# Common pool offsets, a composed pooling matrix, a selection rate of 0.78 and an earlier first load in a one-core encoder block

## The chip, the cores and the metric

The kernel runs on one core of one Trainium2 chip. The metric is the device time of one execution in microseconds (us). Engines are named as in the profile: PE (TensorE: matmuls, and PEld, its weight loads), DVE (VectorE), ACT (ScalarE), POOL (GpSimd) and SP (SyncE, which here only issues DMAs).

## The reference, cut to what matters

One layer of a hybrid encoder block over 2048 tokens of width 1024, in fp32. What the change touches is the pooling branch:

```python
proj = x @ w_in[l]
q, c_kv, q_idx, w_idx, k_idx, pool_in, gate_logits = split(proj)
attn = sparse_indexed_attention(q, k_lat, c_kv, q_idx, w_idx, k_idx)   # top 256 keys per query
branch_a = (attn per head @ w_uv) @ w_attn_branch[l]
# multiscale_pool: per group g of 128 channels, trailing mean over (2,4,8,16)[g] frames minus token
mixed    = einsum('bsgc,gcd->bsgd', pooled, w_pool) * pool_scale
branch_b = mixed @ w_pool_branch[l]
gate_a, gate_b = split(sigmoid(gate_logits))
x = LN(ALPHA*x + (gate_a*branch_a + gate_b*branch_b) @ w_out[l])
x = LN(ALPHA*x + conv_ffn(x))
```

Between the pooled values and `branch_b` there is nothing that is not linear: a 128x128 map per group, a scale per channel, and a 512x1024 matrix.

## The kernel before, in words

**Arithmetic.** Every fp32 operand is split into two fp32r parts, high and low (`split`, `split_new`): either ACT writes the high part and DVE the low part of the whole tile, or POOL does both in pieces of 256 columns. `mm3` (L346) then makes one product of three matmuls: high by high, high by low, low by high. Its second operand is the stationary one or the moving one as the caller wants; in a row of the profile `p<-x,b` the moving operand is in `x`, the stationary one in `b`.

**Stages, in order of time.** Four groups of 512 tokens each pass through `proj_index` (about 0 to 204 us: the indexer's rows and keys), then, in a second round, each group through `proj_pool`, `proj_q` and `proj_gates` (about 204 to 1061 us). Attention over 16 blocks of 128 queries follows (to about 1620 us), then `mix_out` (to about 1900 us), then the feed-forward part in two halves, `up_half` and `down_half` each (to the end).

**The background.** Index scores and the bitwise top-256 selection (`scores_and_selection`) run in the background of the projections. They are generators on the list `bg`; `turn` (L368) is called between pieces of foreground work and takes steps from them while a credit lasts. The credit grows by `RATE` times the modelled PE time that went by, and a step costs the modelled DVE or ACT time that it emits, whichever is more. `widen` (L1124), called in the last gate stage of the last group, emits all that is left of the background at once, releases the pool `wide` that holds the index scores, and opens the pool `more` in the same place. All engines execute in the order in which the program emits; SP issues its DMAs in that order too.

**Weights.** `Weights.get(i)` (L257) hands out the split parts of weight i, loads i+1 and i+2 and splits i+1. In group 0 the parts are split on chip and also stored to a DRAM scratch (`keep`, the DMAs `wp<-b`); groups 1 to 3 load them back from there. Of the splits that may go to POOL every fourth by a running count of all splits (`turns`) goes to ACT and DVE.

**The pooling branch.** `proj_pool` makes the four groups' inputs, `window` their trailing sums on POOL, and `less` the pooled values, split in two. In `tables`, at the start, the 128x128 maps `w_pool` are loaded and split into the tile `wpool`. In `proj_gates`, at the four places `PM_AT` = (4, 5, 6, 7) of the gate loop, `pool_map(k)` (L799) multiplies pooled group k by its map, and ACT and DVE scale and split the result into `self.pm`. Later, for each of four j, 24 matmuls of 512 columns multiply `self.pm` by 256 columns of `w_pool_branch`, whose load and split `self.ab` does like any other weight. So a group has four calls of `pool_map`, three matmuls each.

**Where the tiles lie.** Tiles come from pools that stand one behind the other in each partition's memory. From the left: `const`, `big` (tile name `b`, made by `T`), `mid` (`m`), `sm`, and then `wide` (index scores, `i`) and later `more` (`x`) in the same place. From the right end: `early` (among others `kst`, the indexer's keys), and later `late` (`l`) in its place. As the program before places them, a tile of `big` or `mid` begins at byte 96 modulo 512 in its partition, one of `wide` or `more` at byte 160, `kst` at 416, `wpool`, `cos` and `sin` at 480, and one of `late` at 480. Slices taken of them by the matmuls of the projections, of attention's values, of the mix and of the feed-forward part step by multiples of 512 bytes. The identity matrix used for transposes lies at 128. In `up_half` the weights are in `b`; the activations that they multiply lie, by X_MORE and `x_mix`, in `b`, `x` or `l`.

**The first pool weights.** In `proj_index` of the last group, after the loop over x of its first weight block, `self.ab.split(0)` loads and splits the first two blocks of the pooling projection.

Of the kernel before, what the change touches and what calls it, by code (L numbers as in the profile page):

```python
# [9 lines left out]
F32 = mybir.dt.float32  # L10
F32R = mybir.dt.float32r
# [4 lines left out]
AF = mybir.ActivationFunctionType  # L16
OP = mybir.AluOpType
# [3 lines left out]
P = 128  # L21
NB = S // P
G = 512
NG = S // G
# [48 lines left out]
FINE = "fine"  # L73
PAUSE = "pause"
GRAIN = 1
RATE = 0.75
CAP = 1.5
TAIL = "D--"
ORDER = (3, 2, 1, 6, 5, 4, 7)
# [20 lines left out]
X_MORE = tuple((m, 2) for m in ORDER[:6]) + tuple((m, 3) for m in ORDER[:2])  # L100
LASTK = 8
KEYS_AT = 5
PM_AT = (4, 5, 6, 7)
SCAN = 1.04
PIECE = 256

# [160 lines left out]
class Kern:  # L267
    def __init__(self, ctx, tc, a, out):
        self.clocks = Clocks()
        self.tc, self.nc, self.a, self.out = tc, PacedCore(tc.nc, self.clocks), a, out  # L270
        self.stores, self.older, self.bg, self.late = [], [], [], []
        self.const = ctx.enter_context(tc.tile_pool(name="const", bufs=1))
        self.big = ctx.enter_context(tc.tile_pool(name="big", bufs=34))
        self.mid = ctx.enter_context(tc.tile_pool(name="mid", bufs=8))
        self.sm = ctx.enter_context(tc.tile_pool(name="sm", bufs=4))
        self.early_pool = tc.alloc_tile_pool(name="early", bufs=1, side="right")
        self.wide_pool = tc.alloc_tile_pool(name="wide", bufs=4)
        self.late_pool = self.more_pool = None
        self.p1 = ctx.enter_context(tc.tile_pool(name="p1", bufs=4, space=PSUM))
        self.p2 = ctx.enter_context(tc.tile_pool(name="p2", bufs=2, space=PSUM))  # L280
        self.dram = ctx.enter_context(tc.tile_pool(name="dram", bufs=1, space=bass.MemoryType.DRAM))
        self.n, self.shared, self.turns, self.plain = 0, True, 0, True
        self.credit = self.seen = 0.0
# [119 lines left out]
    def tables(self):  # L403
        nc = self.nc
        posf = self.M([NB, P])
        nc.vector.tensor_copy(posf, self.posi)
        inv = self.E([P, ROT], name="inv")
        for i, f in enumerate(FREQS):
            nc.gpsimd.memset(inv[:, i:i + 1], f)
        pp = self.PS1()  # L410
        nc.tensor.transpose(pp[:, :NB], posf, self.ident[:NB, :NB])
        pos = self.C([P, NB], name="pos")
        nc.vector.tensor_copy(pos, pp[:, :NB])
        self.cos = self.E([P, NB, ROT], name="cos")
        self.sin = self.E([P, NB, ROT], name="sin")
        n = NB * ROT
        ang = self.M([P, NB, ROT])
        nc.vector.tensor_tensor(ang, pos.unsqueeze(2).to_broadcast([P, NB, ROT]),
                                inv[:, None, :].to_broadcast([P, NB, ROT]), op=OP.mult)
        ang = ang.rearrange("p b r -> p (b r)")  # L420
        kf = self.M([P, n])
        for s in (2.0 ** 21, 2.0 ** 10, 1.0):
            nc.vector.tensor_scalar(kf, ang, 1.0 / (2 * math.pi * s), MAGIC, op0=OP.mult, op1=OP.add)
            nc.vector.tensor_scalar(kf, kf, MAGIC, None, op0=OP.subtract)
            for c in TWO_PI:
                nc.vector.scalar_tensor_tensor(ang, kf, -c * s, ang, op0=OP.mult, op1=OP.add)
        for tab, shift in ((self.sin, 0.0), (self.cos, math.pi / 2)):
            r = self.M([P, n])
            nc.vector.tensor_scalar(r, ang, shift, None, op0=OP.add)
            nc.vector.tensor_scalar(kf, r, PI32, -2 * math.pi, op0=OP.is_gt, op1=OP.mult)  # L430
            nc.vector.tensor_tensor(r, r, kf, op=OP.add)
            nc.vector.tensor_scalar(r, r, PI32, -PI32, op0=OP.min, op1=OP.max)
            nc.scalar.activation(tab.rearrange("p b r -> p (b r)"), r, AF.Sin)
        nc.tensor.transpose(pp[:, 16:20], self.psc, self.ident[:4, :4])
        nc.vector.tensor_copy(self.pscale, pp[:, 16:20])
        wp = self.T([P, 4, P])
        nc.sync.dma_start(wp, self.a["w_pool"][0].rearrange("g c d -> c g d"))
        self.wpool = self.E([P, 2, 4, P], F32R, name="wpool")
        self.split(self.wpool[:, 0], self.wpool[:, 1], wp)

    def setup(self):
        nc = self.nc
        self.ident = self.C([P, P], name="ident")
        make_identity(self.tc.nc, self.ident)
        self.mhalf = self.C([P, 1], name="mhalf")
        nc.gpsimd.memset(self.mhalf, -0.5)
        self.ws = self.E([P, NB, IH], name="ws")
        self.kst = self.E([P, S], F32R, name="kst")
        self.halo = self.C([P, 4, HALO], name="halo")
        nc.gpsimd.memset(self.halo, 0.0)  # L450
        self.rcount = self.C([P, HALO], name="rcount")
        for t in range(HALO):
            nc.gpsimd.memset(self.rcount[:, t:t + 1], 1.0 / (t + 1))
        self.pscale = self.C([P, 4], name="pscale")

        self.d_cv = [self.DT([G, DL], name="cv") for _ in range(NG)]
        self.d_xT = [[self.DT([P, 2, 2, G], name="xT") for _ in range(DC // 2)] for _ in range(NG)]
# [108 lines left out]
    def proj_index(self, g, done):  # L566

        nc = self.nc
        rows = [self.T([P, 704]) for _ in range(RB)]
        self.rows[g] = rows  # L570
        for c in range(3):
# [3 lines left out]
            n = 256 if c < 2 else 200  # L575
            if c == 0:
                accs = [self.PS1() for _ in range(RB)]

                def use(pair):
                    for rb in range(RB):  # L580
                        drain(self.proj_r(accs[rb][:, :256], w, rb, 256, [pair]))

                n = 0
                for _ in self.split_x(g, use):
                    if n == (XAT if g else 3) and g + 1 < NG:
                        self.load_x(g + 1)
                    n += 1
                    yield
                if g + 1 == NG:
                    self.ab.split(0)  # L590
                    self.plain = False
                    self.load_parts(0, range(NFIRST))
            for rb in range(RB):
                if c == 0:
                    ps = accs[rb]
                else:
                    if (c, rb) == P1AT and g + 1 < NG:
                        self.split_ahead(g + 1, P1N)
                    ps = self.PS1()
                    yield from self.proj_r(ps[:, :n], w, rb, n)  # L600
                b = g * RB + rb
# [194 lines left out]
        if self.lazy:  # L796
            self.lazy.pop(0)()

    def pool_map(self, k):  # L799
        nc = self.nc  # L800
        t = self.pooled[k]
        ps = self.PS1()
        self.mm3(ps, self.wpool[:, 0, k], self.wpool[:, 1, k], t[:, 0], t[:, 1], True, True)
        o = self.T([P, 2, G], F32R)
        sc = self.pscale[:, k:k + 1]
        nc.scalar.activation(o[:, 0], ps, AF.Identity, scale=sc)
        nc.vector.scalar_tensor_tensor(o[:, 1], ps, sc, o[:, 0].bitcast(F32), op0=OP.mult, op1=OP.subtract)
        self.pm.append(o)

    def proj_gates(self, g):  # L810
        nc = self.nc
        base = g * self.nab + 6
        self.pm = []
        for j in range(4):
            w = self.ab.get(base + j)
            if j == 1:
                self.rope_load(g)
            while self.lazy or j and self.fins:
                self.lazy_step()
            if j == 2:  # L820
                turning = self.rope_turn(g)
            for i in range(2):
                ps = self.PS1()
                for step in self.proj_t(ps, w, i * P):
                    if j == 2:
                        turning.pop(0)()
                    yield step

                def gate(dst=self.d_gm[g][:, 2 * j + i, 0], ps=ps):
                    ga = self.M([P, G])  # L830
                    nc.scalar.activation(ga, ps, AF.Sigmoid)
                    nc.scalar.dma_start(dst, ga)

                self.after(DG, gate)
                if 2 * j + i + 1 in PM_AT:
                    yield 2.6
                    self.pool_map(len(self.pm))
                yield 2.6
        for j in range(4):
            w = self.ab.get(base + 4 + 2 * j)  # L840
# [12 lines left out]
            for i in range(2):  # L853
                ps = self.PS1()
                yield from self.proj_t(ps, w, i * P)

                def gate(ps=ps):
                    gb = self.M([P, G])
                    nc.scalar.activation(gb, ps, AF.Sigmoid)
                    gates.append(gb)  # L860

                self.after(DG, gate)
                if 9 + 2 * j + i in PM_AT:
                    yield 2.6
                    self.pool_map(len(self.pm))
                yield 2.6
            if j == 3 and g + 1 < NG:
                self.load_parts(g + 1, range(NPRE, DC // 2))
# [3 lines left out]
            for i in range(2):  # L872
                ps = self.PS1()
                c0 = i * P
                for k in range(4):
                    self.mm3(ps, wh[:, k, c0:c0 + P], wl[:, k, c0:c0 + P], self.pm[k][:, 0], self.pm[k][:, 1],
                             k == 0, k == 3)
                    if k in FW:
                        yield FINE
# [292 lines left out]
    def scores(self, b, hf):  # L1172
# [8 lines left out]
            del self.qs[b]  # L1181
        N = P * (b + 1)
        npc = (N + 1023) // 1024
        st = self.unit[(b, hf)] = {"p": [], "sum": self.sml([P, 4, 2], tag="ssum", bufs=10), "np": npc}
        cost = 12.0 * N * 0.00042
        for h4 in range(4):
            h = hf * 4 + h4
# [845 lines left out]
```

## Time and profile before

| what | value |
|---|---|
| times of the runs shown | 3251.01, 3256.0, 3257.76 us (median 3256.0) |
| profiled execution, its own time | 3253.0 us |
| its span, first to last instruction | 3251.2 us |
| PE / PEld busy | 3144.5 / 2594.9 us (97% / 80%) |
| DVE / ACT / POOL busy | 2351.4 / 1516.1 / 1238.0 us |
| mean granted PE clock | 0.987 |
| matmuls | 15054 |

Busy times are those of instructions in the trace, and a matmul's end is modelled: two matmuls in a row overlap in it, so PE can be 100% busy and still have matmuls that start later than they could. The distance from one start to the next, or the time of a stretch divided by the number of its matmuls, tells PE's pace. "Idle before" names what an engine waited for before a group of instructions.

### The profile page before, as it was taken

Reading aid. Unit: us, or ns where it says so; the run is one execution under the profiler, and the core shown is the slowest. Engines: PE = TensorE matmul, PEld = TensorE weight load, DVE = VectorE, ACT = ScalarE, POOL = GpSimd, SP = SyncE. Lnnn points to the kernel's source line nnn. Section 1 sums busy time; section 2 is a strip of 40 time slices with the busy share of each in tenths; the row PEclk is TensorE's granted clock in tenths of the full one; section 3 lists DMA queues with packets and bytes.
Section 4 is the critical chain, followed back from the end, with each engine's and each line's share of the span. In section 5 each row is a group of like instructions: output and inputs, shape, how many; then the busy total and the mean of one; then the engine's idle time right before and its main releaser. Section 6 shows DMA issues by size and latency. Waiting matters only on the chain.

```text
span 3251.2 us, 44226 instructions
## 1 busy us (share of the span) xinstructions
PE 3144.5 (97%) x15054; PEld 2594.9 (80%) x15054; DVE 2351.4 (72%) x3947; ACT 1516.1 (47%) x2338; POOL 1238.0 (38%) x1262
## 2 busy tenths in 40 slices
PE   8899899999999899999999999999999999999998
PEld 8887787888888788888778877777878778887786
DVE  4589868978998777777676576666678955555788
ACT  3467547836774666666511133333344522222442
POOL 4126411020010877776631143343176611111663
PEclk9999999999999999999999999999999999999999
DMA  8558855853866444443554358998897666666984
GB/s 302 179 188 291 308 189 206 319 194 126 297 218 221 148 164 140 167 167 138 180 207 162 132 207 311 336 336 295 296 367 256 234 245 243 238 242 232 352 281 163
DMA packets 331809, 753.94 MB, mean 232 GB/s; under 512 B 32122, under 2 KB 117054, under 8 KB 331582
## 3 DMA queue, kind: packets, MB, share of 16 engines
q1 hardware_dynamic: 322774, 735.36, 63.6%
q10 hardware_dynamic: 8808, 15.74, 1.3%
q8 instruction: 119, 1.95, 0.2%
q14 instruction: 108, 0.88, 0.1%
HBM read 518.56 MB, written 232.42 MB: 231 GB/s over the span
## 4 chain that ended last, share of the span: by engine, by line
PE 75%; DVE 10%; DMA 5%; POOL 4%; issue 4%; ACT 2%; SPq 0%; DVEq 0%; ACTq 0%; POOLq 0%
PE p L160 75%; DVE b L160 4%; DVE m L160 3%; POOL b L160 1%; ACT b L160 1%; DMA b<-h 1%; POOL x L160 1%; DMA b<-in_w_ffn_down_dram 1%; POOL l L160 1%; ACT m L160 1%; DMA wp<-b 1%; POOL m L160 1%; DVE h L160 1%; DMA b<-in_w_in_dram 0%; DMA b<-xT 0%
## 5 line engine op out<-in xcount | busy, mean ns | idle before, releaser
L160 PE MATMUL p<-b,b 128*128 128x512 f32 (+2 forms) x9284 | 2231.2, 380 | 67.5 <-DVE b L160 25.2
L160 PEld LDWEIGHTS p<-b,b 128*128 128x128 f32 x9284 | 1647.1, 190 | 403.4 <-DVE b L160 37.4
L160 ACT ACTIVATE b<-p 128x512 fp32r<-128x512 f32 (+9 forms) x662 | 403.8, 634 | 632.7 <-PE p L160 595.8
L160 ACT ACTIVATE b<-b 128x1024 fp32r<-128x1024 f32 (+2 forms) x255 | 261.3, 1029 | 411.1 <-POOL b L160 155.8
L160 DVE TENSOR_TENSOR b<-b,b 128x1024 fp32r<-128x1024 f32 (+4 forms) x261 | 364.0, 1425 | 74.4 <-ACT b L160 67.6
L160 PE MATMUL p<-x,b 128*128 128x512 f32 x1440 | 384.2, 395 | 0.8 <-DVE m L160 0.8
L160 ACT ACTIVATE m<-i,F 128x1536 int8<-128x1536 f32 (+4 forms) x224 | 316.8, 1416 | 65.3 <-DVE F L160 35.7
L160 PEld LDWEIGHTS p<-x,b 128*128 128x128 f32 x1440 | 271.5, 189 | 63.4 <-DVE m L160 1.2
L160 DVE TENSOR_SCALAR_CACHE_REDUCE m<-i,F 128x1152 int8<-128x1152 f32 (+7 forms) x238 | 314.6, 1338 | 1.2 <-DMA gm<-m 0.3
L160 DVE TENSOR_TENSOR m<-m,p 128x512 f32<-128x512 f32 x176 | 120.2, 684 | 263.9 <-ACT b L160 199.1
L160 POOL TENSOR_TENSOR b<-b,b 128x256 fp32r<-128x256 f32 (+3 forms) x212 | 238.7, 1140 | 99.8 <-ACT b L160 91.1
L160 POOL TENSOR_TENSOR m<-b,b 128x512 f32<-128x512 f32 x99 | 137.9, 1401 | 339.6 <-issue 262.0
L160 DVE SCALAR_TENSOR_TENSOR b<-b,cw,b 128x1023 f32<-128x1023 f32 (+1 forms) x176 | 242.9, 1388 | 14.0 <-ACT b L160 13.2
L160 DVE TENSOR_TENSOR b<-p,b 128x512 fp32r<-128x512 f32 (+1 forms) x286 | 201.2, 713 | 69.3 <-ACT b L160 66.8
L160 POOL TENSOR_TENSOR b<-b,m 128x512 f32<-128x512 f32 x110 | 190.4, 1744 | 137.1 <-DMA m<-in_w_ffn_down_dram 85.4
L160 PE MATMUL p<-b 128*128 128x512 f32 x616 | 234.5, 393 | 4.4 <-ACT b L160 3.7
L160 PE MATMUL p<-b,x 128*128 128x512 f32 (+3 forms) x864 | 228.1, 394 | 2.6 <-DVE mx L160 1.6
L160 DVE CUSTOM_DVE_ANT_0 b<-p,b 128x1024 f32<-128x1024 f32 (+7 forms) x192 | 174.1, 909 | 72.9 <-PE p L160 67.4
L160 ACT ACTIVATE m<-p 128x512 f32<-128x512 f32 (+1 forms) x188 | 110.2, 591 | 199.9 <-PE p L160 194.7
L160 PE MATMUL p<-ident,b 128*128 128x128 f32 x1328 | 196.7, 275 | 2.8 <-DVE b L160 1.6
L160 ACT ACTIVATE b<-b,mx 128x1024 f32<-128x1024 f32 (+7 forms) x192 | 171.5, 896 | 53.6 <-DVE mx L160 52.3
L160 DVE SCALAR_TENSOR_TENSOR i<-b,ws,i 128x768 f32<-128x768 f32 (+5 forms) x154 | 159.0, 1061 | 50.3 <-ACT b L160 47.3
(145 smaller groups left out, 3032.7 us busy)
## 6 DMA issues: line engine op xcount, KB each, us to landing
b<-uw SPq DMA_DIRECT2D x308, 512.0 KB, 6.3
b<-wp SPq DMA_DIRECT2D x192, 512.0 KB, 6.1
uw<-l SPq DMA_DIRECT2D x98, 512.0 KB, 3.0
b<-in_w_ffn_down_dram SPq DMA_DIRECT2D x154, 256.0 KB, 5.2
b<-h SPq DMA_DIRECT2D x154, 256.0 KB, 5.3
wp<-b SPq DMA_DIRECT2D x64, 512.0 KB, 6.0
uw<-b SPq DMA_DIRECT2D x56, 512.0 KB, 4.5
h<-m SPq DMA_DIRECT2D x110, 256.0 KB, 5.7
```

Source lines behind the costliest of these rows:

```text
L160: return f(*args, **kw)
```

## The change

Four things are changed together. (1) A pool `edge` with one tile of 384 bytes is placed at the right end, a tile `end` of 448 bytes is added to `early`, and a tag of `sm` gets 8 buffers of 32 bytes where it had 10. (2) `pool_map` is dropped. `w_pool` is loaded in the first gate step of group 0 (`pool_load`), transposed on PE, scaled and split (`pool_turn`); in each of the four j of group 0, `compose` multiplies it into the 256 columns of `w_pool_branch` that are next, in 12 matmuls of 256 columns, and ACT and DVE split the product, which takes the place of the weight. The branch matmuls of all groups then multiply the pooled values by the product; groups 1 to 3 load it back from the scratch. (3) `RATE` is 0.78, it was 0.75. (4) The first pool weights are loaded (not split) before the loop over x of the last `proj_index`.

```diff
-RATE = 0.75
+RATE = 0.78
-PM_AT = (4, 5, 6, 7)
@@ Kern.__init__
+        self.edge = ctx.enter_context(tc.tile_pool(name="edge", bufs=1, side="right"))
         self.early_pool = tc.alloc_tile_pool(name="early", bufs=1, side="right")
@@ tables
-        wp = self.T([P, 4, P])
-        nc.sync.dma_start(wp, self.a["w_pool"][0].rearrange("g c d -> c g d"))
-        self.wpool = self.E([P, 2, 4, P], F32R, name="wpool")
-        self.split(self.wpool[:, 0], self.wpool[:, 1], wp)
@@ setup
+        edge = self.edge.tile([P, 96], F32, tag="edge", name="edge")
+        nc.gpsimd.memset(edge, 0.0)
...
         self.kst = self.E([P, S], F32R, name="kst")
+        nc.gpsimd.memset(self.E([P, 112], name="end"), 0.0)
...
+        self.wpool = self.E([P, 2, 4, P], F32R, name="wpool")
@@ proj_index
             if c == 0:
                 accs = [self.PS1() for _ in range(RB)]
+                if g + 1 == NG:
+                    self.ab.load(0)
@@ in place of pool_map
+    def pool_load(self):
+        self.wp = self.T([P, 4, P])
+        self.nc.sync.dma_start(self.wp, self.a["w_pool"][0].rearrange("g c d -> c g d"))
+
+    def pool_turn(self):
...
+        for k in range(4):
+            nc.tensor.transpose(ps[:, k], self.wp[:, k], self.ident)
+        for k in range(4):
+            sc = self.pscale[:, k:k + 1]
+            nc.scalar.activation(t[:, 0, k], ps[:, k], AF.Identity, scale=sc)
+            nc.vector.scalar_tensor_tensor(t[:, 1, k], ps[:, k], sc, t[:, 0, k].bitcast(F32),
+                                           op0=OP.mult, op1=OP.subtract)
+
+    def compose(self, i):
+        (wh, wl), = self.ab.parts[i]
+        hi, lo = self.T([P, 4, 256], F32R), self.T([P, 4, 256], F32R)
+        for c in range(2):
+            ps = self.PS1([P, 2, 256])
+            for n in range(2):
+                k = 2 * c + n
+                self.mm3(ps[:, n], self.wpool[:, 0, k], self.wpool[:, 1, k], wh[:, k], wl[:, k], True, True)
+            cs = slice(2 * c, 2 * c + 2)
+            nc.scalar.activation(hi[:, cs], ps, AF.Copy)
+            nc.vector.tensor_tensor(lo[:, cs], ps, hi[:, cs].bitcast(F32), op=OP.subtract)
+        self.ab.parts[i] = [(hi, lo)]
@@ proj_gates, first half (j, i)
+            if g == 0 and j == 0:
+                self.pool_load()
...
-                if 2 * j + i + 1 in PM_AT:
-                    yield 2.6
-                    self.pool_map(len(self.pm))
+                if g == 0 and (j, i) == (1, 0):
+                    self.pool_turn()
@@ proj_gates, second half (j, i)
-                if 9 + 2 * j + i in PM_AT:
-                    yield 2.6
-                    self.pool_map(len(self.pm))
+                if g == 0 and i == 0:
+                    self.compose(base + 5 + 2 * j)
...
-                    self.mm3(ps, wh[:, k, c0:c0 + P], wl[:, k, c0:c0 + P], self.pm[k][:, 0], self.pm[k][:, 1],
+                    self.mm3(ps, wh[:, k, c0:c0 + P], wl[:, k, c0:c0 + P], self.pooled[k][:, 0], self.pooled[k][:, 1],
                              k == 0, k == 3)
@@ scores
-        st = self.unit[(b, hf)] = {"p": [], "sum": self.sml([P, 4, 2], tag="ssum", bufs=10), "np": npc}
+        st = self.unit[(b, hf)] = {"p": [], "sum": self.sml([P, 4, 2], tag="ssum", bufs=8), "np": npc}
```

More of the change, by code (lines that the diff above doesn't have):

```diff
@@ L797, in lazy_step @@
             self.lazy.pop(0)()
-    def pool_map(self, k):
+    def pool_load(self):
+        self.wp = self.T([P, 4, P])
+        self.nc.sync.dma_start(self.wp, self.a["w_pool"][0].rearrange("g c d -> c g d"))
+    def pool_turn(self):
         nc = self.nc
[L801 to L808, printed above, removed]
+        ps = self.PS1([P, 4, P])
+        t = self.wpool
+        for k in range(4):
[5 more added lines that the diff above has]
+                                           op0=OP.mult, op1=OP.subtract)
+        self.wp = None
+    def compose(self, i):
+        nc = self.nc
+        (wh, wl), = self.ab.parts[i]
[9 more added lines that the diff above has]
+        self.ab.parts[i] = [(hi, lo)]
     def proj_gates(self, g):
@@ L812, in proj_gates @@
         base = g * self.nab + 6
-        self.pm = []
         for j in range(4):
             w = self.ab.get(base + j)
+            if g == 0 and j == 0:
+                self.pool_load()
             if j == 1:
```

## The prediction

> **What bounds the kernel now.** I read the page first, then the chain of waits in order of time, then PE's timeline where the chain stays on PE, and last the waits around the edges of the stages. Of the page one line, the shares of the chain that ended last:
>
> ```profile
> PE 75%; DVE 10%; DMA 5%; POOL 4%; issue 4%; ACT 2%; SPq 0%; DVEq 0%; ACTq 0%; POOLq 0%
> ```
>
> PE sets the time, so its pace and its waits are all that counts. The chain, in order of time (start, length, number of instructions), shows the pace:
>
> ```profile
> 26.09 80.01 PE p L160 x681
> ...
> 1649.82 175.32 PE p L160 x755
> ...
> 2617.69 386.14 PE p L160 x1660
> ...
> 3059.42 111.38 PE p L160 x490
> ```
>
> All but the first are stretches of 512-column matmuls. In the second down half one takes 111.38/490 = 227.3 ns. In the second up half it takes 386.14/1660 = 232.6 ns, in the mix 175.32/755 = 232.2. The shapes are the same. PE's timeline inside the second up half, and at the step into the down half, shows what differs:
>
> ```profile
> 2746.16 1.55 PE L160 MATMUL p<-b,b 128*128 128x512 f32 x6
> 2747.55 1.55 PE L160 MATMUL p<-x,b 128*128 128x512 f32 x6
> ...
> 3015.85 0.39 PE L160 MATMUL p<-l,b 128*128 128x512 f32 x1
> 3016.08 0.85 PE L160 MATMUL p<-b,b 128*128 128x512 f32 x3
> 3016.77 0.40 PE L160 MATMUL p<-b 128*128 128x512 f32 x1
> ...
> 3021.77 0.62 PE L160 MATMUL p<-b,b 128*128 128x512 f32 x2
> 3022.22 0.39 PE L160 MATMUL p<-b 128*128 128x512 f32 x1
> 3022.45 0.62 PE L160 MATMUL p<-b,b 128*128 128x512 f32 x2
> ```
>
> From start to start: where the moving operand alternates between pools, even matmuls with both operands in `b` take (2747.55-2746.16)/6 = 232 ns. After the last `l` the pace is first (3016.77-3016.08)/3 = 230, and in the pure stretch (3022.45-3021.77)/3 = 226.7. So the loss isn't in the pool `x` itself: it follows each step from one pool to another and lasts some matmuls beyond it. The pools differ in their offset modulo 512 (96, 160, 480). Tiles inside `b` lie 4096 bytes apart over more than 130 KB, so distance alone, at equal offset, doesn't show it.
>
> **The change part by part.** *Offsets.* Reckoned from the places before: `late` goes to 480-384 = 96, `kst` to 416-384-448, again 96 modulo 512, `wide` and `more` to 160-64 = 96. All matmuls of mix and feed-forward then have one offset. Their number:
>
> ```profile
> L160 PE MATMUL p<-x,b 128*128 128x512 f32 x1440 | 384.2, 395 | 0.8 <-DVE m L160 0.8
> L160 PE MATMUL p<-b,x 128*128 128x512 f32 x744 | 206.2, 404 | 0.4 <-DVE mx L160 0.4
> L160 PE MATMUL p<-l,b 128*128 128x512 f32 x396 | 104.4, 403 | 9.2 <-DVE b L160 9.2
> ```
>
> An up half has 22x7x12 = 1848 matmuls, so at 232.6-227.3 = 5.3 ns each at most 9.8 us. I take 9.3 for the second half, and 7 for the first, whose stretches are short and broken by waits after which PE must find its pace again. Mix: at most 755 x (232.2-227.3) = 3.7; only half its moving operands lie in `x`; I take 2.5. Attention: the 744 matmuls with stationary `x`, at most 744 x 5.3 = 3.9; transposes, whose identity stays at 128, come every few matmuls and break the pace anyway; I take 2.5. Keys in `kst`: 0.7, since slices that start at odd multiples of 256 bytes stay off. Sum 22, between 0 (the offset is not the cause) and 28. A loss I exclude: the new offset is the one at which the fast stretches run.
>
> The Trainium skill speaks against this part. In "TensorE: Matmul & The Clock Gate", Part 2, "Step-by-step: what each phase is for", it says that PE has two independent read ports, and that loading the next weights does not steal read bandwidth from the running matmul; by that, an offset between operands is worth nothing. By this rule the sum below would be 22 us higher; by the rows it is as stated.
>
> *Composed matrix.* Out go 48 matmuls of `pool_map`, and in group 1 the waits that come with it:
>
> ```profile
> L160 PE MATMUL p<-b,wpool x48: 392/398/404, 309.5 to 990.0; 128*128 128x512 f32 x48
> ...
> L160 PE MATMUL p<-b,b 128*128 128x256 f32 x960 | 127.8, 290 | 14.8 <-ACT b L160 8.7 <-DVE b L160 3.2 <-POOL b L160 2.7
> ...
> L160 PE MATMUL p<-ident,b 128*128 128x128 f32 x1328 | 196.7, 275 | 2.8 <-DVE b L160 1.6 <-issue 0.9 <-ACT b L160 0.2
> ...
> PE p L160 <- ACT m L160: 5.4, 3, 4.0
> ```
>
> At 227.3 ns they are 10.9 us. In come 4x12 matmuls of 256 columns at 127.8/960 = 133 ns, 6.4 us, and four transposes of 196.7/1328 = 0.15 us: a net 3.9 us less. The 5.4 us (PE's waits from 500 to 700 us) arise because ACT, full of selection passes, is late to empty PSUM, of which each `pool_map` takes a buffer; without it the gates alone hold them, and I count all 5.4 as gone. ACT and DVE lose `pool_map`'s 16 passes each, which lay beside PE's work.
>
> New is that `compose` needs the split weight one gate step (24 matmuls, 5.4 us) earlier than the branch did, in PE's order, so all matmuls queue behind it. In group 0:
>
> ```profile
> 334.76 33.94 PE L160 MATMUL p<-b,b 128*128 128x512 f32 x149
> ...
> 343.50 1.27 DVE L160 TENSOR_TENSOR b<-b,b 128x1024 fp32r<-128x1024 f32 x1 [0.17 <-ACT b L160]
> ...
> 376.37 34.28 PE p L160 x142
> ...
> 400.81 1.51 POOL L160 TENSOR_TENSOR b<-b,b 128x256 fp32r<-128x256 f32 x2
> ```
>
> The stretch of 149 is 5 + 48 + 24 + 48 + 24, so the first `compose` would stand at 334.76 + 29 x 0.227 = 341.3 us; the split ends at 344.8: 3.5 us late. The last one would stand at 376.37 + 94 x 0.227 = 397.7, the split ends at 402.3: 4.6 late. The first delay pushes PE toward a stall that stands at 368 to 376 us anyway and is partly lost in it. I take 4 us, between 0 and 10. The product's own evacuation (ACT, DVE) has the next gate step as cover; without it 1 to 2 us each. Every fourth split changes engine, because one split less is counted: zero, within 4 us either way. Part: -3.9 - 5.4 + 4 = -5.3.
>
> *Rate.* What is left over at the end of the last group is emitted at once by `widen`, and PE meets it:
>
> ```profile
> 1050.76 1.89 ACT L160 ACTIVATE b<-i,tn 128x1920 f16<-128x1920 f32 x1
> 1052.73 1.60 POOL L160 TENSOR_SCALAR x<-b 128x256 fp32r<-128x256 f32 x2 [24.17 <-ACT b L160]
> ...
> 1054.87 4.57 DVE L160 TENSOR_TENSOR_SCAN b<-b 128x1920 f16<-128x1920 f16 x1
> ...
> 1065.09 0.66 PE L160 MATMUL p<-b,b 128*128 128x128 f32 x4 [3.81 <-DVE b L160]
> ...
> PE p L160 <- DVE b L160: 3.8, 1, 3.8
> PE p L160 <- DVE mx L160: 2.6, 4, 1.5
> PE p L160 <- POOL b L160: 1.4, 2, 1.0
> ```
>
> POOL's first split into `x` waits for ACT's last read of `i`, DVE's splits stand behind a selection tail, of which the row of 1054.87 is the last long scan, and PE waits for these (last rows: its waits from 1044 to 1130 us). 0.03 more credit over the 829 us from 216 to 1045, at 0.2153 modelled (L142) for 0.227 real, is 23 us of work, less about 4 for modelled PE time that is gone with `pool_map`: more than a tail of about 15 us. DVE then splits at once, and POOL starts 7 or 8 us sooner. I take 7, between 8 (the three rows of waits) and -3.
>
> *First load.* Now:
>
> ```profile
> 145.65 5.77 DMA b<-in_w_in_dram
> ...
> 156.46 0.98 ACT L160 ACTIVATE b<-p 128x640 f32<-128x640 f32 x2 [4.70 <-POOL b L160]
> 161.27 1.51 ACT L160 ACTIVATE b<-p 128x768 f32<-128x768 f32 x2 [3.84 <-POOL b L160]
> ...
> PE p L160 <- ACT b L160: 6.4, 2, 3.5
> ```
>
> The load lands at 151.4, POOL splits until 161, and ACT's score tiles wait for buffers that POOL still reads; PE waits 6.4 us for ACT (its waits from 150 to 165 us). Issued one weight block earlier, by some 12 us, the load lands and is split before ACT needs these buffers; On SP it passes some stores of scratch and one load of an index row, each of which moves back by the two issues of this load, under 2 us; the scores have that much in hand. It holds two buffers of `big` for those 12 us more. Between 0 and 6.4, I take 5. The load of `w_pool` leaves the start, where PE runs without a break (26.09, 80.01 us), so nothing; in group 0 it is asked for three gate steps, some 16 us, ahead of its transposes, and in SP's order its one issue delays what follows by under 1 us.
>
> **Sum.** 22 + 5.3 + 7 + 5 = 39.3. Against the profiled execution's own 3253.0 us this gives 3213.7; the median of the runs shown is 3.0 above that one, so 3217.
>
> **The rivals.** (a) Offset without effect; for it, another stage may be slower for another reason, its many short accumulations say; against it, the return to 226.7 ns within some ten matmuls of the last foreign operand. 3217 + 22 = 3239. This is the result of the skill's rule on read ports, too.
>
> (b) Offsets and first load come, but group 0's new waits (10 in place of 4) and a selection that ends no sooner take the rest. The 5.4 us of waits for ACT stay, so the composed matrix costs -3.9 + 10 = 6: 3256 - 22 - 5 + 6 = 3235. For it: POOL works in order, and its last split above ends 4.6 us after the place where PE would want it; against it, the stall at 368 to 376 takes up part of what comes before.
>
> (c) Slower: at 0.78 the selection outruns DVE and ACT, and PE waits for gate evacuations behind it.
>
> ```profile
> 560.00:700.00 140.00, 139.09 (x606) 114.97 (x607) 128.97 (x303) 90.07 (x122) 19.74 (x28) 0.99 0.71 260
> 780.00:1030.00 250.00, 250.00 (x1102) 205.27 (x1101) 231.28 (x414) 179.01 (x202) 14.10 (x21) 1.00 0.63 228
> 290.00:420.00 130.00, 117.69 (x495) 95.31 (x494) 111.47 (x294) 71.39 (x131) 63.08 (x109) 0.95 0.89 325
> ```
>
> DVE is at 128.97/140 = 92% and 231.28/250 = 93%. Four per cent more selection, less the passes of `pool_map`, makes 94 to 95: it fits. If the idle 7% cannot be filled, since a selection pass waits for the decision of the one before, the 4% come back as waits over 755 us: 30 us, and the granted clock falls with waits (0.95 from 290 to 420, 6.5 us of 130), some 15 more, and the 7 of the rate are lost: 3256 - 32 + 45 = 3269. It decides from the point where DVE's idle share is all chain.
>
> (d) All four small and cancelling: about 3253.
>
> **How the numbers follow.** Forecast 0.62 (3200 to 3232 by its bounds), (a) 0.12, (b) 0.16, (c) 0.06, (d) 0.04. Range 3198 to 3244: it holds forecast, (a) and (b). About 0.2% is what a measurement of this kernel can tell from no change. Faster by more: 0.62 + 0.12 + 0.16, less tails, 0.88; within: 0.05; slower: 0.07.
>
> **What would show it.** Offsets: the second up half at 227 ns a matmul (about 377 us for 1660) where it is 232.6; if it stays, (a). Composition: no PE wait for ACT at 550 to 561; waits before 256-column matmuls in group 0. Rate: POOL's first split into `x` with no long scan on DVE beside it, and PE unbroken there; DVE over 95% with PE waits for ACT or DVE between 560 and 1030 would be (c). First load: no ACT wait for POOL at 156 and 161. The prediction is wrong if the span is above 3241 or if the feed-forward part isn't shorter by 10 us or more.

## The result

| | before | changed | |
|---|---|---|---|
| median (6 executions each) | 3255.0 us | 3230.1 us | ratio 0.9915 [0.9905, 0.9925] |
| profiled execution, own time | 3253.0 us | 3230.6 us | -22.4 us |
| PE busy | 3144.5 us | 3123.2 us | -21.3 us |

The change makes the kernel faster by 24.9 us in the medians (27.7, between 24.4 and 30.9, by the ratio and its interval). The forecast was 3217, 39 us less than before. The total is inside the predicted range and on its slow side; the terms of the sum are another matter.

The changed kernel's page, its span and its busy times:

```profile
span 3228.8 us, 44242 instructions
PE 3123.2 (97%) x15058; PEld 2590.6 (80%) x15058; DVE 2352.2 (73%) x3941; ACT 1511.3 (47%) x2332; POOL 1245.5 (39%) x1272
```

PE still sets the time. Where the 22 us went is read by lining up the same foreground matmul in both traces and following the difference of its start: -0.8 us at the first pool projection (204 us); +31.3 where group 1's projections start (410.5 before, 441.8 after), of which some 8 are 32 score matmuls and 16 transposes that now come ahead of this point; +9.1 where group 2's start, +5.7 where group 3's start; +1.8 just ahead of attention; -8.4 twenty microseconds into it; -8.2 at its end; -10.1 at the end of the mix; -17.8 at the end of the first up half, -16.1 where the second starts; -21.1 at its end; -22.4 at the end. So group 0 takes, and the later groups, attention's start and the two up halves give. The busy times by stage say the same; columns are the stretch in us, its length, then for PE, PEld, DVE, ACT and POOL the busy us with the number of instructions, then the granted clock, the DMA share and GB/s. The kernel before:

```profile
204.00:432.00 228.00, 210.06 (x895) 169.65 (x894) 194.57 (x542) 136.25 (x257) 118.87 (x208) 0.96 0.83 297
432.00:1040.00 608.00, 601.17 (x2710) 493.92 (x2709) 522.82 (x958) 401.36 (x504) 50.58 (x65) 1.00 0.60 215
1040.00:1130.00 90.00, 80.95 (x431) 68.40 (x429) 66.08 (x173) 50.55 (x118) 70.57 (x75) 0.92 0.48 150
```

The changed kernel, the same stretches:

```profile
204.00:432.00 228.00, 197.66 (x827) 154.78 (x825) 196.24 (x538) 136.91 (x261) 121.57 (x208) 0.93 0.75 266
432.00:1040.00 608.00, 608.00 (x2762) 503.98 (x2762) 520.39 (x952) 393.67 (x487) 52.31 (x68) 1.00 0.63 226
1040.00:1130.00 90.00, 86.84 (x484) 73.60 (x483) 62.40 (x178) 53.22 (x127) 75.69 (x80) 0.98 0.53 167
```

From 204 to 432 us PE now idles 30 us of 228 where it idled 18, and its granted clock is 0.93 instead of 0.96. From 432 to 1040 it has no gap at all (608.00 of 608.00). From 1040 to 1130 it idles 3 us instead of 9. What PE waited for, changed kernel, first from 200 to 432 us (us in total, times, longest):

```profile
PE p L159 <- ACT m L159: 11.3, 6, 3.9
PE p L159 <- POOL b L159: 9.8, 9, 5.1
PE p L159 <- ACT b L159: 5.0, 3, 2.2
```

Then from 140 to 170 us (first two rows) and from 1040 to 1130 us:

```profile
PE p L159 <- DVE b L159: 2.9, 1, 2.9
PE p L159 <- ACT b L159: 1.1, 1, 1.1
...
PE p L159 <- POOL b L159: 1.6, 2, 1.0
PE p L159 <- DVE mx L159: 1.4, 4, 0.4
```

**The pace.** The chain of waits inside the second up half is now one piece that runs on into the down half (start, length, number of matmuls):

```profile
2594.04 406.07 PE p L159 x1771
```

That is 229.3 ns a matmul. Of the second up half alone, the 1661 from the place where the prediction's stretch starts took 386.2 us before and take 380.7 now, 229.2 ns each against 232.5. PE's timeline shows both what was gained and what is missing:

```profile
2727.66 1.52 PE L159 MATMUL p<-x,b 128*128 128x512 f32 x6
2729.02 1.52 PE L159 MATMUL p<-b,b 128*128 128x512 f32 x6
2730.38 1.52 PE L159 MATMUL p<-x,b 128*128 128x512 f32 x6
...
2748.06 2.50 PE L159 MATMUL p<-b,b 128*128 128x512 f32 x10
2750.40 1.54 PE L159 MATMUL p<-x,b 128*128 128x512 f32 x6
2751.78 0.62 PE L159 MATMUL p<-b,b 128*128 128x512 f32 x2
```

At 2729 the operand changes pool every six matmuls, and one takes (2730.38-2729.02)/6 = 226.7 ns: the pace of the pure stretches. In the ten from 2748.06 stands one interval of 277 ns, and the six after them still take (2751.78-2750.40)/6 = 230. There are 30 such short stalls, of 277, 338 (with 262 just ahead of it) and 328 ns in turn, three in every 168 matmuls (38.5 us). After each the intervals go 236, 228, 233, 231 and the like for four to ten matmuls before they are 226.7 again. Ten times the excess of one turn (50 + 35 + 111 + 101 ns) is 3.0 us, and the matmuls behind the stalls cost some 40 ns a stall, 1.2 us: together these are the 4.2 us between 380.7 and 1661 x 226.7 = 376.5. The trace shows no wait at them. The kernel before has its long intervals at the same 30 matmuls, of 254, 335 and 284 ns on a pace of 232, so they are not new.

**Group 0.** The changed kernel's timeline (in brackets the idle time before the row and what ended it):

```profile
336.88 0.95 PE L159 MATMUL p<-b,wpool 128*128 128x256 f32 x6 [0.66 <-ACT m L159]
341.00 0.58 ACT L159 ACTIVATE m<-p 128x512 f32<-128x512 f32 x1
341.72 1.62 PE L159 MATMUL p<-b,wpool 128*128 128x256 f32 x6 [3.89 <-ACT m L159]
345.46 0.58 ACT L159 ACTIVATE m<-p 128x512 f32<-128x512 f32 x1
346.10 14.13 PE L159 MATMUL p<-b,b 128*128 128x512 f32 x50 [2.76 <-ACT m L159]
...
384.10 0.37 POOL L159 MEMSET c<- 128x4 f32 x1 [14.63 <-DVE cg L159]
384.75 3.99 PE L159 MATMUL p<-b,b 128*128 128x512 f32 x8 [5.13 <-POOL b L159]
```

The first `compose` waits not for a weight, as I had reckoned, but for ACT's gate evacuations (`m<-p`, 341.00 and 345.46), which free the PSUM buffers it needs and which stand on ACT behind selection passes (`m<-i,F`, without a gap from 337.1 to 346.0): 0.66 + 3.89 + 2.76 = 7.3 us. Forty microseconds later POOL stands 14.63 us at a small memset of the selection that waits for DVE; the weight split queued behind it is late, and PE waits 5.13 us for that.

**The edge of attention.** The rows that answer to those of 1052.73 and 1054.87:

```profile
1039.30 5.07 POOL L159 TENSOR_SCALAR x<-b 128x256 fp32r<-128x256 f32 x2 [7.31 <-ACT b L159]
1039.94 4.23 DVE L159 TENSOR_TENSOR_SCAN b<-b 128x1920 f16<-128x1920 f16 x1
```

DVE's last long scan comes 14.9 us sooner and POOL's first split into `x` 13.4 us sooner, while the projections' last matmuls lie 1.8 us later: the selection is done in time.

### The profile page after: what moved, and what is told of

The parts are those of the page before. It is cut to its first block, busy times and chain, and to the rows that moved or that the text cites. A ratio compares the mean times of both kernels' runs of the same rounds, so it can differ in the third digit from the quotient of the medians.

```text
span 3228.8 us, 44242 instructions
## 1 busy us (share of the span) xinstructions
PE 3123.2 (97%) x15058; PEld 2590.6 (80%) x15058; DVE 2352.2 (73%) x3941; ACT 1511.3 (47%) x2332; POOL 1245.5 (39%) x1272
## 5 line engine op out<-in xcount | busy, mean ns | idle before, releaser
L159 ACT ACTIVATE b<-p 128x512 fp32r<-128x512 f32 (+8 forms) x670 | 409.5, 634 | 624.3 <-PE p L159 599.0
L159 DVE TENSOR_TENSOR b<-b,b 128x1024 fp32r<-128x1024 f32 (+7 forms) x261 | 369.1, 1446 | 74.5 <-ACT b L159 60.8
L159 DVE SCALAR_TENSOR_TENSOR b<-b,cw,b 128x1023 f32<-128x1023 f32 (+1 forms) x176 | 243.1, 1389 | 13.0 <-ACT b L159 12.2
```

The lines of the kernel that those rows point to most:

```text
L159: return f(*args, **kw)
```

## The experiments

Each run is compared with runs of the kernel before on the same chip; a ratio is given with its 95% interval. Changes in us are (1 - ratio) x 3256. Where the expectations speak of group 0's end, they mean its last `compose` (422.9 us in the changed kernel) or, where there is none, its last branch matmul (410.2 us before). These are not the same matmul, and the "13 us by which group 0 now ends later" are their difference; the readings below use the start of group 1's projections, found by counting the projection and branch matmuls (410.5 and 441.8 us). PE doesn't keep to the order of the program's text everywhere: at 420.12 us two matmuls of 512 columns stand inside the changed kernel's last `compose`. So such a place is good to a few matmuls.

**1. Four parts, each alone.**

The offsets alone:

```diff
+        self.edge = ctx.enter_context(tc.tile_pool(name="edge", bufs=1, side="right"))
+        edge = self.edge.tile([P, 96], F32, tag="edge", name="edge")
+        nc.gpsimd.memset(self.E([P, 112], name="end"), 0.0)
-        ... tag="ssum", bufs=10
+        ... tag="ssum", bufs=8
```

> The kernel before with the common offset alone. Theory A (each step between pools of different offset costs PE its pace for some ten matmuls): the second up half at 229 ns a matmul as in the changed kernel (before: 232.6), the two up halves together 13 us shorter, mix 2, attention 1 to 2, so 15 to 19 us less in all, ratio 0.994 to 0.9955. Rival B (the faster up halves come from the other work arriving at other times): the second up half stays at 232 ns, less than 3 us in all.

Measured: median 3240.4, ratio 0.9951 [0.9939, 0.9962], 16.0 us less (12.4 to 19.9), as theory A has it. The chain's piece in the second up half, which the prediction shows with 386.14 us for the kernel before:

```profile
2615.02 380.58 PE p L160 x1660
```

That is 229.3 ns a matmul, the changed kernel's pace. This part is most of the gain. Not all of the 16 us has a place in the trace: the two up halves are 5.5 us shorter each, the mix 0.5, and attention is 1.0 longer. The two traces differ by 9.0 us in all, because the profiled execution is 3.6 above this kernel's median and that of the kernel before lies 3 below its own.

The composed matrix alone, at rate 0.75 and with the old places and load:

```diff
-        self.pool_map(len(self.pm))
+        self.pool_load() ... self.pool_turn() ... self.compose(base + 5 + 2 * j)
```

> The kernel before with the composed matrix alone, rate 0.75. Theory A (the loss of group 0 is compose's own: its PSUM buffers wait for ACT behind selection passes): PE waits for ACT around the first 256-column matmuls at 335 to 350 us, group 0 ends 8 to 14 us later than before, groups 1 to 3 win back 13 to 14 (5.4 of waits, 36 matmuls), so between 6 us less and 1 us more. Rival B (the loss is the rate's): no waits of PE for ACT there over 1 us, group 0 ends within 3 us, 10 us less in all.

Measured: median 3254.6, ratio 0.9992 [0.9984, 1.0001], 2.6 us less (5.2 less to 0.3 more). Group 1's projections start 14.8 us later than before, group 2's 2.7 later, group 3's 0.6 earlier; the last matmuls ahead of attention lie 3.4 us earlier, and those twenty microseconds into it 2.2 later. At its first `compose` PE waits 3.5 us for ACT (at 343.9), as theory A says and rival B doesn't. Its rows at the edge (POOL's first split into `x`, and PE's longest wait from 1040 to 1130 us):

```profile
1054.73 1.61 POOL L159 TENSOR_SCALAR x<-b 128x256 fp32r<-128x256 f32 x2 [34.91 <-ACT b L159]
...
PE p L159 <- DVE b L159: 10.9, 1, 10.9
```

By the rule of the credit, fewer matmuls mean less of it for the background; more selection is left over, and PE waits 10.9 us in one piece at attention's start. So this part alone gives its gain back there.

The rate alone:

```diff
-RATE = 0.75
+RATE = 0.78
```

> The kernel before with the rate 0.78 alone. Theory A: group 0 ends within 4 us of before; the start of attention, as of its second block, comes 7 to 10 us earlier because POOL's splits no longer wait for the selection's tail; 6 to 10 us less in all. Rival B (0.78 is more than ACT and DVE can take in): waits of PE for ACT in groups 0 and 1, group 0 10 us later, no gain in all.

Measured: median 3257.4, ratio 1.0001 [0.9992, 1.0010], nothing within 3.3 us. The edge behaves as forecast: PE's waits from 1040 to 1130 us fall from 8.9 to 1.4 us, and the same matmul gains 10.3 us across it. But group 1's projections start 19.1 us later than before, and most of that, 15.3 us, is still there just ahead of attention. From 200 to 432 us PE waits 32.6 us where it waited 17.8. First the largest of these waits, then what stands at the end of its longest piece:

```profile
PE p L160 <- DVE b L160: 16.7, 4, 12.1
...
377.56 1.05 ACT L160 ACTIVATE b<-b 128x1024 fp32r<-128x1024 f32 x1
...
387.16 0.10 POOL L160 MEMSET c<- 128x4 f32 x1 [12.97 <-DVE cg L160]
...
391.32 1.21 DVE L160 TENSOR_TENSOR b<-b,b 128x1024 fp32r<-128x1024 f32 x1
...
392.59 2.92 PE L160 MATMUL p<-b,b 128*128 128x512 f32 x6 [12.09 <-DVE b L160]
```

PE gets on when DVE has written the low part of a weight (391.32). ACT's part of a split of this size was written at 378.6; in between DVE is busy, for the most part with selection passes. Beside this POOL stands at the same memset of the selection as in the changed kernel, but here that isn't what PE waits for. So rival B, that 0.78 is more than the other engines can take in, is right on group 0 and on the sum, with DVE in place of ACT. In group 0 DVE and POOL also split the new weights; there the faster selection costs what it saves at the edge.

The early load alone:

```diff
                 accs = [self.PS1() for _ in range(RB)]
+                if g + 1 == NG:
+                    self.ab.load(0)
```

> The kernel before with the earlier first load alone. Theory A (what the load sets free at 150 to 162 us, the next waits take up, as in the changed kernel, where the first pool projection starts 0.8 us sooner): 0 to 2 us less. Rival B (the 5 us of my sum are there and something else in the changed kernel takes them): the first pool projection starts 4 to 6 us sooner and the whole is 4 to 6 us shorter.

Measured: median 3251.5, ratio 0.9986 [0.9977, 0.9995], 4.6 us less (1.6 to 7.5). Its profile shows the load issued at 130 us instead of 146 and POOL's split ended at 151.3 instead of 161.2; ACT's waits for POOL at 156 and 161 are gone. PE, though, meets a new wait there:

```profile
154.05 1.94 PE L160 MATMUL p<-ident,b 128*128 128x128 f32 x8 [4.92 <-DVE b L160]
```

The 6.6 us for ACT between 140 and 170 us have become 4.9 for DVE, and the first pool projection starts only 0.5 us sooner (0.8 in the changed kernel). The profiled execution took 3258.2 us, 6.7 above this kernel's median, so it may not be typical; why the median gains more than this trace shows stays open.

The four single effects add up to 22.9 us less; together they are 24.4 to 30.9. Within the intervals the parts add.

**2. Which offset, and by how much.** The changed kernel with a narrower block at the right end, which shifts the down weights' tiles `l` and the keys' store against all others:

```diff
-        edge = self.edge.tile([P, 96], F32, tag="edge", name="edge")
+        edge = self.edge.tile([P, 80], F32, ...)   # 64 bytes off
+        edge = self.edge.tile([P, 64], F32, ...)   # 128 bytes off
+        edge = self.edge.tile([P, 32], F32, ...)   # 256 bytes off
```

> The changed kernel with the right-hand pools 64 bytes off (edge 320 bytes: the tiles of l, kst and the other early tiles at 160 modulo 512, all else at 96). Theory A (it is the step between offsets that costs, some 50 ns spread over the ten matmuls after it): in the second up half only one of seven products uses l, nine matmuls per unit, so per unit 9 slow matmuls and some ten slow ones after the step back: 2 us per half, the half at 230.1 to 230.6 ns a matmul (changed kernel 229.1, before 232.6); the matmuls of b right after the last l at 228 to 236 ns. Rival B (what counts is the pool or its place in memory, not the offset): l and all else at 226 to 227 ns as in the changed kernel, half at 229.1. Rival C (matmuls with operands in the off pool are slow themselves, those after them not): 0.9 us per half, b at 226.7 at once.

> The changed kernel with the block at the right end 64 columns wide in place of 96, so that the down weights and the keys' store lie 128 bytes off all other operands. 64 bytes off cost (second up half 381.45 us, 229.7 ns a matmul, tiles of the last weights at 231.8), 256 bytes off cost nothing (380.64 us, 226.7). Theory A, the offset counts modulo 256: 128 off costs like 64: second up half 381.2 to 381.8 us, matmuls with the shifted operand at 231 to 232 ns, and the first ten after the last of them at 230 to 236. Theory B, it counts modulo 128: 380.4 to 380.8 us and 226.7 ns throughout. Nothing of the computation is left out.

> The same with the right-hand pools 256 bytes off (edge 128 bytes: l and kst at 352 modulo 512). If the period is 512 bytes, as kst slices at odd multiples of 256 bytes seemed to say: as with 64 bytes off, 230 to 230.6 ns in the second up half. If it is 256 bytes or less: 229.1 ns, and l at 226 to 227 ns.

Measured, one execution each: the second up half takes 381.45 us at 64 bytes off, 381.37 at 128, 380.64 at 256, and 380.68 in the changed kernel; the intervals of matmuls with `l` average 231.8, 232.4, 226.7 and 226.7 ns. From 2000 us on, one row of the groups of each: 64 off, 128 off, 256 off, in this order (the mean is of modelled durations, which overlap):

```profile
L159 PE MATMUL p<-l,b 128*128 128x512 f32 x351 | 92.0, 401 | 7.8 <-DVE b L159 7.7
...
L159 PE MATMUL p<-l,b 128*128 128x512 f32 x351 | 92.3, 402 | 7.8 <-DVE b L159 7.8
...
L159 PE MATMUL p<-l,b 128*128 128x512 f32 x351 | 90.3, 396 | 7.7 <-DVE b L159 7.7
```

The same instructions, moved by 64 or 128 bytes, take 5 ns longer; moved by 256 they don't. After a run of nine `l` at 64 off the intervals run 234, 231, 233, 236, 224, 231, 236, 228, 233, 230, then 226.7, though all operands then lie at 96: a step of the offset costs up to ten matmuls. At 128 off only five are slow behind such a run (230, 236, 228, 233, 230), and none behind the last, single `l`, where the expectation had ten. Whether the offset also costs while it lasts, no stretch of `l` is long enough to tell. At 64 off, theory A's slow matmuls after the step are there, but the half is only 0.8 us longer, which is rival C's size and not A's 2. That the offset is the cause of the slower pace is shown. All other tiles that these matmuls read lay at 96 in these runs, so whether the difference of two offsets counts or the place itself, they don't tell; the slow matmuls that follow, themselves at 96, speak for the difference. The prediction reckoned offsets modulo 512; modulo 256 is what the three runs and the row of the changed kernel agree with.

**3. The identity matrix.** The changed kernel with the identity of the transposes at 96 instead of 128:

```diff
-        self.ident = self.C([P, P], name="ident")
+        self.ident = self.edge.tile([P, P], F32, tag="ident", name="ident")
```

> The changed kernel with the identity matrix of the transposes moved from offset 128 to 96, the offset of the other operands. Theory A: in attention the transposes break the pace of the matmuls beside them because their moving operand lies 32 bytes off, so that attention (1130 to 1640 us) gets 2 to 5 us shorter: median 3225 to 3228. Theory B, the transposes are short matmuls with limits of their own and the stretches between them too short for an even pace: attention the same within 1 us, median 3229 to 3231. It tells where the predicted 2.5 us of attention went. Nothing of the computation is left out.

Measured: median 3227.4, ratio 0.9913 [0.9900, 0.9926], not to be told from the changed kernel (0.9915). Attention, from 1130 to 1640 us, is the same within 0.2 us. The median lies in theory A's range, but the stage on which the theories differ hasn't moved, so theory B holds: attention's pace isn't set by this offset. (That leaves the first reason that the prediction gave, broken stretches, but doesn't show it.)

**4. Where group 0's waits come from.** The product of `compose` in one PSUM tile of two buffers instead of two of one, so that it isn't held by a gate's buffer:

```diff
-        for c in range(2):
-            ps = self.PS1([P, 2, 256])
+        ps = self.PS2([P, 4, 256])
```

> The changed kernel with compose's product in one tile of the other PSUM pool (two banks, used by the index scores only), so that it takes no buffer that the gates use. Theory A (compose's waits for ACT come from PSUM buffers): the waits of PE for ACT m between 330 and 350 us (7.3 us in the changed kernel) go, 3 to 7 us less in all. Rival B (PE is behind what POOL and DVE deliver in group 0, and meets the same time at the next wait): group 0 ends within 2 us of the changed kernel's, the whole within 2 us.

Measured: median 3229.2, ratio 0.9919 [0.9904, 0.9934]: no gain. The waits of 7.3 us from 328 to 352 us are gone, but PE waits longer elsewhere, 6.7 us in one piece for ACT right behind them (at 352.1): group 2's projections start at 655.0 us (654.8 in the changed kernel), and the last matmuls ahead of attention lie 0.3 us later than there. From 200 to 432 us:

```profile
PE p L159 <- ACT b L159: 12.8, 6, 6.7
PE p L159 <- POOL b L159: 4.7, 7, 2.2
```

So the buffer was where PE met the delay, not its cause, as rival B has it.

The rate by group, 0.70 in group 0 and 0.80 later:

```diff
-        self.credit = min(self.credit + RATE * (pe - self.seen), CAP)
+        self.credit = min(self.credit + self.rate * (pe - self.seen), CAP)
...
+            self.rate = 0.7 if g == 0 else 0.8
```

> The changed kernel with the rate 0.70 in group 0 of the second round and 0.80 in groups 1 to 3. Theory A (the rate costs in group 0, where POOL, ACT and DVE also split weights, and pays only at the start of attention): PE's waits from 200 to 430 us fall from 31 us to 15 to 22, those at 1040 to 1130 stay under 6, none over 2 in between; 6 to 12 us less than the changed kernel, ratio to the kernel before 0.988 to 0.990. Rival B (what is not done in group 0 comes back as waits in groups 1 to 3 or in the tail): waits of PE over 5 us between 432 and 1130, no gain over the changed kernel.

Measured: median 3227.6, ratio 0.9910 [0.9893, 0.9926], not to be told from the changed kernel, where theory A had 6 to 12 us less. Group 1's projections start at 419.3 us, 22.5 sooner than in the changed kernel, so the rate is a cause of group 0's delay; group 2's start 7.2 sooner. But 6.6 us of waits come back from 432 to 1040 us and 9.0 from 1040 to 1130, and just ahead of attention the kernel is some 4 us behind the changed one. The largest of them is at the edge:

```profile
PE p L159 <- DVE mx L159: 7.1, 4, 5.9
```

Selection not done in group 0 is owed later, as rival B has it. Both together, with 0.70 and 0.83:

```diff
+        ps = self.PS2([P, 4, 256])
+            self.rate = 0.7 if g == 0 else 0.83
```

> The changed kernel with each composed matrix in one PSUM tile, and the selection at rate 0.70 in group 0 and 0.83 from group 1 on. Theory A, the 13 us by which group 0 now ends later are the price of too fast a selection there alone, and the later groups can take it back: group 0 ends at 408 to 412 us, waits of PE from 432 to 1040 under 2 us, the attention's start 8 to 12 us sooner than in the changed kernel, median 3217 to 3222. Theory B, selection not done in group 0 has to be paid later, as waits of PE for ACT and DVE from 432 to 1130 us (15 us in the run with 0.70 and 0.80): median 3226 to 3231. Nothing of the computation is left out.

Measured: median 3223.8, ratio 0.9904 [0.9890, 0.9917]; the lowest median of all, 6.3 us below the changed kernel's, though the intervals overlap. Its last `compose` ends at 401 us instead of 423, and group 1's projections start at 409.3, where they start at 410.5 in the kernel before. From 204 to 432 us (first row) PE is busy 211.5 us at a clock of 0.96; from 432 to 1040 us it waits for ACT again (second row):

```profile
204.00:432.00 228.00, 211.50 (x924) 172.15 (x925) 193.59 (x532) 133.12 (x254) 118.44 (x211) 0.96 0.83 298
...
PE p L159 <- ACT m L159: 8.3, 5, 3.5
```

The lead over the changed kernel is 12.2 us where group 2's projections start, 6.1 at group 3's and 4.2 ahead of attention, and 9.5 at the end. The result lies between the two theories: group 0 ends as theory A has it, or sooner, and the later waits are theory B's, 15.6 us from 432 to 1130; the median lies between both ranges. In these runs moving the credit between groups is worth a few microseconds at most, since the sum of the selection stays the same.

## Why the prediction was right and wrong

**Bound.** Right: PE sets the time. The 21.3 us that its busy time lost stand beside 22.4 of the profiled time.

**Offsets, 22 us.** The mechanism is right, and rival (a) is out: the run with the offsets alone gives 16.0, and moving one kind of tile by 64 bytes brings the slow pace back. The Trainium skill, "TensorE: Matmul & The Clock Gate", Part 2, "Step-by-step: what each phase is for", says that PE has two independent read ports, by which the offset would be worth nothing. The trace disagrees with what I drew from it: 231.8 against 226.7 ns for one and the same matmul.

The size was wrong by 6 us, in two terms above all. The step "second up half, 9.3" measured 5.5 (5.0 to 5.7 over the whole half): it took every matmul above 227.3 ns for a loss by offsets, but some 4 us of it belong to the 30 short stalls and the matmuls behind each, which don't hang on offsets: the kernel before has them at the same places. The mean of a long stretch was charged to one cause, where the list of its intervals would have shown two. The step "attention, 2.5" measured nothing in the whole: 8.4 us ahead near its start, 8.2 at its end. The matmuls that it named did get faster. From 1130 us to the end of attention, 474 intervals between matmuls with stationary `x` average 230.3 ns in the two kernels with the new offsets and 233.2 to 233.3 in the kernel before and the three single parts without them. That is worth 1.4 us, too little to stand out of a stage whose length varies by 3 us among the four traces without the offsets. The first up half, forecast at 7, shows 7.7 between the two traces and 5.5 with the offsets alone; it holds waits that vary, and the three single parts without the new offsets are 0.7 to 3.0 shorter there, too. The mix shows 1.9 for 2.5, but 0.5 with the offsets alone and up to 1.5 without them, so its gain isn't shown. The keys' term (0.7) can't be seen by itself; its reason, that slices at odd multiples of 256 bytes "stay off", is wrong by the run at 256 bytes.

**Composed matrix, -5.3.** Measured alone: -2.6 (-5.2 to +0.3). The waits at 500 to 700 us went as forecast; PE has none there, and it is this part that removes them: 0.7 us of PE's waits are left from 432 to 1040 us with it alone, 6.1 with the rate alone. What failed is the step "I count all 5.4 as gone" taken together with "the next gate step as cover": `compose` asks for PSUM buffers too, in group 0, where ACT is as late with the gates as it was in group 1, and 7.3 us of the same wait stand there (3.5 with this part alone). The delay that I did price, weights split too late, came later and through POOL (5.13 us at 384.75), where the selection's memset stands ahead of the split.

**Rate, -7.** Measured alone: nothing. In the trace the edge gave what was forecast (7.5 us less waiting, 10.3 in position). The step that failed is the working itself: "0.03 more credit" was set only against the tail that it removes, and its price was looked for over 560 to 1030 us, in rival (c). There it costs nothing, as the forecast had it: the 19.1 us of group 1's start don't grow afterwards. It costs in group 0, where DVE and POOL split weights for the first time: DVE's part of a split stands behind selection passes (12.1 us of PE's waiting with the rate alone), and POOL's splits behind a memset that waits for DVE. Rival (c) had the right mechanism in the wrong stage, so that the price was 15 us and not 45. The rows for it were on the page before: the row of 290 to 420 us, which I quoted for its clock, shows PE busy 117.69 of 130, so that stage already had waits to be lengthened. No run takes the rate alone out of the changed kernel: what 0.78 is worth beside the composed matrix, which at 0.75 leaves 10.9 us of waiting at attention's start, isn't measured.

**First load, -5.** The median gains 4.6 (1.6 to 7.5), as forecast, and the split ends before ACT needs its buffers, as forecast. But the trace doesn't show the gain at the place named: a wait of 4.9 us for DVE stands where 6.6 for ACT stood, and the pool projection starts 0.5 to 0.8 us sooner. The size agrees; the way is not shown, so that the term came out right may be luck.

**The rivals.** The measured 3230 lies nearer to (b), 3235, than to the forecast's 3217: group 0's new waits did take some of the rest, 12.8 us more (30.6 against 17.8) where the sum had 4 and (b) had 10. But (b) also held that the selection would end no sooner and that the waits for ACT at 500 to 700 us would stay, and both are wrong. The forecast's condition for being wrong, a feed-forward part that is not shorter by 10 us, didn't come: it is shorter by 12 (from -10.1 to -22.4).

## What to carry to other kernels

When PE is the bound and its matmuls are all alike, list the intervals from start to start before looking for waits: a pace that is a few per cent off in busy stretches is worth more than most gaps, and the place of the tiles in memory can be its cause. Give each excess interval one cause before multiplying a mean by a count. When background work is sped up, price it in every stage that shares its engines, first where those engines also have one-time work, and not only at the end where the saving lies.

## What was not expected of the hardware

In this kernel PE's pace for fp32r matmuls of 512 columns settles at 226.7 ns, and a disturbance costs more than itself: after a stall of 50 to 110 ns, or a run of moving operands 64 or 128 bytes off modulo 256, four to ten matmuls take 224 to 241 ns (mean 231) until the pace is back, 20 to 60 ns in all. An operand 256 bytes off does nothing of the kind. A stationary operand 64 bytes off costs as well, 233.3 against 230.3 ns in attention. What makes the slow matmuls, and what the 30 regular stalls of the second up half are, no run here shows.
